# Block sums of the MLP: ended earlier, turned by VectorE and DMA instead of TensorE, with the last down tiles in other PSUM banks and the norm's column sums later

## The chip, the cores and the metric

One core of a Trainium2 chip runs the whole program as one launch. The metric is the device time of that launch in microseconds (us). A profiled execution gives the span from the first to the last instruction, a row for every instruction on every engine, and the waits between them. The engines are TensorE (matmuls; "PE" in the profile, its weight loads "PEld"), VectorE ("DVE"), ScalarE ("ACT"), GpSimd ("POOL", which here only fills buffers and issues DMAs) and SyncE ("SP", which issues the weight loads from memory).

## The reference

A decoder trunk of two layers over 256 positions and 2048 channels, in float32. Layer 0 mixes by dilated attention, layer 1 by sparse attention. Behind each mixer stands an MLP, and behind that a gated embedding ("PLE"):

```python
hn = rmsnorm(h, mlp_norm_g[i])
h = h + jnp.square(jax.nn.relu(hn @ mlp_w1[i])) @ mlp_w2[i]
gate = jax.nn.sigmoid(rmsnorm(h, ple_norm_g[i]) @ ple_w_gate[i])
h = h + (p[i] @ ple_w_proj[i]) * gate
```

The MLP has 8192 hidden channels. The norm divides each position by the root of the mean of its squares over the channels, so it needs a sum over all 2048 channels. At the end a last norm follows.

## The kernel before

**Layout.** The residual stream lies in 16 tiles x[0..15], each 128 channels by 256 positions (channels on the partitions). Every float32 weight is split into a rounded high part and a rest, "whi" and "wlo"; so are the activations. A product is then made of three: high by high, high by low, low by high. ScalarE makes whi (line 281), VectorE wlo (line 308).

**Chunks.** The work is a list of chunks of weights (128 x 1024), written out in order by the program itself; no scheduler reorders it. At each chunk Program.run (line 118) issues, in this order: loads of later chunks on SP, ScalarE's whi of the chunk four ahead, VectorE's wlo of the chunk three ahead, then one stage of every follow-up that is under way (advance(), line 83), then the chunk's matmuls. A follow-up is a Python generator; each `yield` ends a stage. After `yield "tensor"` it goes on behind the matmuls of that chunk. Each engine takes its instructions in the order in which they are issued.

**The MLP** (mlp, line 592). "Up" tiles make 128 hidden channels each; "down" tiles make 128 of the first 1024 output channels from 2048 hidden ones, two chunks a tile. The last 1024 output channels are made by a scheme of seven products of half blocks in place of eight (seven_products, line 649): 32 steps j in three parts, "AD", "B" and "C", which are strewn between the tiles by the loop at line 755. Seven PSUM banks, acc[1..7], collect them over the whole MLP; acc[0] is the one bank that all tiles after the fourth share (mono, line 603). finish (line 684) adds the seven banks to four block sums c11, c21, c12, c22, which have positions on the partitions and channels along the row; they have to be turned to be added to x[8..15].

**PSUM** has four single banks, tag "mm", and two double banks, tag "at" (lines 208 to 212). A slot is given to a new tile of its tag when all instructions of the tile that holds it are behind it, later ones of the program included; of the free slots the one that came free first is taken.

**The end of an MLP.** finish has these stages, one per chunk: the copies of p1 and p5 and the sums u (lines 690 to 693); c11 and c21; c22 and c12; behind the matmuls of that chunk sixteen 128 x 128 turns on TensorE into both double banks (line 708); two stages on, four adds of 128 x 512 to x[8..15] (line 714); then, two tiles a stage, renorm (line 430): high part and squares on ScalarE, low part and the sum of squares on VectorE. Two down-tile chunks follow the last product, then one chunk of the embedding's projection, then the eight chunks of the first gate quarter, of which chunk c needs x[2c] and x[2c+1] as activations.

**The norm behind it** (Norm.factor, line 374) is started after gate chunk 4. When all 16 tiles are summed it issues, each a stage apart: the column sums on TensorE (line 347), the root on VectorE and ScalarE (lines 354 and 355), the inverse and two diagonals on VectorE (lines 361 to 367), and, in layer 0, the spread over all partitions on TensorE (line 371, into the tile of the column sums) and a copy on ScalarE (line 389). In layer 0 the gate quarters are quads, which take four single banks and both double banks in turn (four_banks, line 470); the column sums use a double bank when the quad before used single ones:

```python
ps = banks2()[:, 0, :] if parity[0] else bank()
...
rp = self.spread(ps)
```

Quarter 0 of the gates uses the single banks, the projection of quarter 1 (one chunk) both double banks, quarter 1 the single ones again. In layer 1 (last_ple, line 776) positions are the rows of the gates; column sums and projections use single banks, nothing is spread, and turn (line 782) turns x in four quarters by VectorE's 32 x 32 block transposes and DMAs through memory (regroup, line 312, on GpSimd's queue: one write of 512 KB, then four reads of 128 KB, each of which waits for the write).

Of the kernel before, what the change touches and what calls it, by code (L numbers as in the profile page):

```python
# [10 lines left out]
F32 = mybir.dt.float32  # L11
# [4 lines left out]
P = 128  # L16
D = 2048
T = 256
# [12 lines left out]
ROPE_SWAP = [(j + 16) % 32 for j in range(32)]  # L31

TURN_STAGES = 7
WARM_UP = 9
DMA_AHEAD = 7
DMA_AHEAD_LATER = 10
# [8 lines left out]
def f32(ap):  # L45
    return ap.bitcast(F32)
# [121 lines left out]
def kernel(ctx: ExitStack, tc: tile.TileContext, a: dict, out: bass.AP):  # L168
# [20 lines left out]
    def flip(*args):  # L189
        twos[0] = 4  # L190
        nc.tensor.transpose(*args)  # L191
# [19 lines left out]
    def banks2():  # L211
        return pspool.tile([P, 2, 512], F32, tag="at", name="at", bufs=2)
# [99 lines left out]
    def regroup(dst, src):  # L312

        moved = dram.tile([P, 4, 256], F32, tag="pm", name="pm")
        nc.gpsimd.dma_start(moved, src)
        for b in range(4):
            nc.gpsimd.dma_start(dst[32 * b:32 * b + 32], moved[:, b].rearrange("(a r) x -> r a x", a=4))

    class Norm:
# [51 lines left out]
            mm(ps[:, 128:128 + T], ones, self.diag, start=True, stop=True)  # L371
            return ps[:, 128:128 + T]

        def factor(self, roped=False, spread=True):
            while self.done < KT:
                yield
            yield "tensor"
            ps = self.column([self.acc])
            yield
            self.root(ps)  # L380
            yield
            self.invert()
            if not spread:
                return
            yield "tensor"
            rp = self.spread(ps)
            yield
            r = stat.tile([P, T], F32, tag="sr", name="sr", bufs=1)
            nc.scalar.copy(r, rp)
            if roped:  # L390
                yield
                self.rc = stat.tile([P, T], F32, tag="rc", name="rc", bufs=1)
                self.rs = stat.tile([32, T], F32, tag="rs", name="rs", bufs=1)
                inner, table = (lined, residues) if roped == "residues" else (lined, lined)
                nc.vector.tensor_mul(inner(self.rs), inner(r[:32, :]), table(ropeS))
                nc.vector.tensor_copy(self.rc, r)
                nc.vector.tensor_mul(inner(self.rc[:32, :]), inner(r[:32, :]), table(ropeC))
            self.r = r
# [102 lines left out]
    def single(src, acts, done, mid=(), ring=bank, one_half=False):  # L501

        st = []
        for c in range(2):
            def step(hi, lo, c=c):
                if c == 0:
                    st.append(ring())
                    if ring is not bank:
                        twos[0] = 4
                tiles = [(st[0], i * P, have(acts, 8 * c + i), c + i == 0, 8 * c + i == KT - 1) for i in range(8)]  # L510
                if one_half:
                    for ps, col, rhs, first, end in tiles:
                        three(ps[:, :T], hi, lo, col, rhs, first, end)
                else:
                    mm_tiles(hi, lo, tiles)
                return [done(st[0])] if c else []
            prog.chunk(src(c), step)
            if c == 0:
                for fn in mid:
                    prog.op(fn)  # L520
# [71 lines left out]
    def mlp(layer, xg, norm, to, norm2, pg):  # L592
# [10 lines left out]
        def mono():  # L603
# [5 lines left out]
                acc.extend(bank() for _ in range(4))  # L609
            return acc[{1: 2, 3: 3, 4: 4}.get(opened[0], 0)]  # L610

        def up_done(k, ps, alone=True):
            if alone:
                s = halves(ps)
                t = tmp.tile([P, T], F32, tag="et", name="et", bufs=7)
                nc.vector.tensor_add(t, s[:, :T], s[:, T:])  # L616
            else:
                t = sum_halves(ps)
            yield
            while norm.r is None:  # L620
                yield
            nc.vector.scalar_tensor_tensor(t, t, 0.0, norm.rb, op0=ALU.max, op1=ALU.mult)
            yield
            nc.scalar.activation(t, t, AF.Square)
            ht = cur["h"].tile([P, 2 * T], F32R, tag="h", name="h", bufs=H_BUFS)
            yield from split_to(ht, t)
            h[k] = ht
            kept[k] = t
            if k % 2 == 0:
                return  # L630
            yield
            one, two = kept.pop(k - 1), kept.pop(k)
            a11, a21, a12, a22 = one[:, :P], one[:, P:], two[:, :P], two[:, P:]
            s = cur["h"].tile([P, 2 * T], F32, tag="ew", name="ew", bufs=3)
            d1, s2, s3, s4 = (s[:, i * P:(i + 1) * P] for i in range(4))
            nc.vector.tensor_sub(d1, a21, a22)
            nc.vector.tensor_sub(s3, a11, a21)
            nc.vector.tensor_sub(s2, d1, a11)
            nc.vector.tensor_add(s4, a12, s2)
            if k > 1:  # L640
                yield
            sh = cur["h"].tile([P, 2 * T], F32R, tag="fh", name="fh", bufs=5)
            nc.scalar.copy(sh, s)
            yield
            sl = cur["h"].tile([P, 2 * T], F32R, tag="fl", name="fl", bufs=5)
            nc.vector.tensor_sub(sl, s, f32(sh))
            forms[k // 2] = sh, sl
# [35 lines left out]

        def finish():
            p3, p5, p7, p6, p1, p2, p4 = acc[1:]
            c = cur["h"].tile([P, 2 * CH], F32, tag="r7", name="r7", bufs=R7_BUFS)
            c11, c21, c12, c22 = (c[:, i * 512:(i + 1) * 512] for i in range(4))
            u = cur["h"].tile([P, CH], F32, tag="T", name="T", bufs=1)
            s = cur["h"].tile([P, 2 * CH], F32, tag="r7", name="r7", bufs=R7_BUFS)[:, :512]
            nc.scalar.copy(c11, p1)  # L690
            nc.scalar.copy(s, p5)
            nc.vector.tensor_add(u[:, :512], p6, c11)
            nc.vector.tensor_add(u[:, 512:], p7, u[:, :512])
            yield
            nc.vector.tensor_add(c11, p2, c11)
            nc.vector.tensor_add(c21, p4, u[:, 512:])
            yield
            nc.vector.tensor_sub(c22, s, u[:, 512:])
            nc.vector.tensor_add(c12, p3, s)
            nc.vector.tensor_sub(c12, c12, u[:, :512])  # L700
            yield "tensor"
            flat = []
            for n in range(2):
                flat.append(banks2().rearrange("p a b -> p (a b)"))
                for i in range(4):
                    for m in range(2):
                        src = c[:, (2 * n + m) * 512 + i * P:(2 * n + m) * 512 + (i + 1) * P]
                        flip(flat[n][:, (2 * i + m) * P:(2 * i + m + 1) * P], src, ident)
            yield
            yield  # L710
            for n in range(2):
                for i in range(2):
                    y = xp[4 + 2 * n + i]
                    nc.vector.tensor_add(y, flat[n][:, i * 512:(i + 1) * 512], y)
            begun = []
            for k in range(8, KT + 2, 2):
                for g in begun:
                    for _ in g:
                        pass
                begun = [renorm(i, G_PLE + layer, to, norm2) for i in (k, k + 1) if i < KT]  # L720
                for g in begun:
                    next(g)
                yield
# [13 lines left out]
        def down(b, f):  # L737
            base = layer * 64 + 2 * (b * 8 + f)
            single(lambda c: a["w2d"][base + c], Shifted(h, b * KT), lambda ps: down_done(b, f, ps),
                   ring=mono)  # L740

        quad(lambda c: a["w1"][layer * 128 + c], KT, xg, lambda f, ps: up_done(f, ps, False),
             {4: [norm.factor]}, late=True)
# [5 lines left out]
        parts = [(j, n) for j in range(32) for n in ("AD", "B", "C")]  # L749
        made = {("u", k): -3 for k in range(4)}  # L750
        made.update((what, n) for n, what in enumerate(order))
        first, last = 3, len(order) - 2
        ready = [3 * sum(made["u", 2 * j + 1] <= n - 3 for j in range(32)) for n in range(last + 1)]
        done = downs = 0
        for n, what in enumerate(order):
# [7 lines left out]
                continue  # L763
            spare = min(ready[m] - (m - n) for m in range(n, last + 1) if ready[m] < len(parts) or m == n)
            downs += what[0] == "d"
            even = n - first + 1 + (len(parts) - (last - first + 1)) * downs // (NFB * 8 - 3)
            upto = max(done + 1, min(even, spare)) if n < last else len(parts)
            while done < min(upto, len(parts)):
                j, which = parts[done]
# [6 lines left out]
    def last_ple(layer, pg, xg, norm):  # L776
# [5 lines left out]
        def turn():  # L782
# [3 lines left out]
            e["sq"] = stat.tile([P, 2, 12], F32, name="squares", bufs=1)  # L786
            to = [cur["h"].tile([P, 2 * CH], F32, tag="r7", name="r7", bufs=R7_BUFS) for _ in range(2)]
            for q in range(4):
                for _ in range((1, 3, 3, 11)[q]):
                    yield  # L790
                blocks = cur["h"].tile([P, CH], F32, tag="T", name="T", bufs=1)
                blocks = blocks.rearrange("p (b j k r) -> p b j k r", b=4, j=2, k=4)
# [153 lines left out]
        def gates(q):  # L946
            token_major(lambda c: a["w_gate"][layer * 32 + q * 8 + c], xg,
                        lambda j, ps: gate_done(q, j, ps),
                        {4: [lambda: norm.factor(spread=False)]} if q == 0 else None, banks2 if q else bank)

        prog.op(turn)
        for q in range(2):
# [27 lines left out]
    def ple(layer, pg, xg, norm, nxt, norm2):  # L980
# [34 lines left out]
        for q in range(4):  # L1015
# [12 lines left out]
                prog.op(lambda: parity.__setitem__(0, 0))  # L1028
            else:
                quad(lambda c, q=q: a["w_proj"][layer * 4 + q], 2, pg, proj_done)  # L1030
            hooks = {4: [norm.factor]} if q == 0 else {}
            if q == 3:
                for c in range(6):
                    hooks[c] = [lambda k=k: split_x(k, G_KV, nxt) for k in (2 * c, 2 * c + 1)]
# [721 lines left out]
```

## Time and profile before

| what | us |
|---|---|
| median of 3 runs | 2455.29 |
| lowest, highest | 2454.28, 2455.57 |
| the profiled execution, whole | 2456.09 |
| its span, first to last instruction | 2454.1 |
| TensorE busy in the span | 2443.0 |
| VectorE busy | 2012.8 |
| ScalarE busy | 1507.4 |
| GpSimd busy | 41.9 |

A row of the timelines gives the start in us from the start of the span, the duration in us, the engine, the line of the kernel, the operation, the tile written and those read, their shape, and how many instructions are merged. In square brackets stands how long the engine was idle before, and what released it. Durations of neighbouring matmuls overlap, since they are pipelined; the pace is read from start to start.

### The profile page before, as it was taken

The page shows a single profiled execution, that of the slowest core. Times are in us where ns is not written, and L with a number is a line of the kernel's source. Part 1 is how long each engine was busy: PE and PEld are TensorE (multiplying, and loading weights), DVE is VectorE, ACT ScalarE, POOL GpSimd, SP SyncE. Part 2 cuts the span into 40 slices and gives each one's busy share as a digit, 9 for nine tenths or more (in the row PEclk, how much of TensorE's full clock was granted, in tenths as well). Part 3 has the DMA queues.
Part 4 walks back from the last instruction along what each step waited for, and adds up shares of the span by engine and source line. Part 5 has one row for each costly group of instructions (what it writes and reads, how often), then busy time and mean ns, then how long its engine had stood idle before and what let it go on. Part 6 is the DMA issues. An engine that isn't in the chain of part 4 may idle for free.

```text
span 2454.1 us, 36853 instructions
## 1 busy us (share of the span) xinstructions
PE 2443.0 (100%) x13557; PEld 2117.7 (86%) x13557; DVE 2012.8 (82%) x3562; ACT 1507.4 (61%) x2372; POOL 41.9 (2%) x80
## 2 busy tenths in 40 slices
PE   9999999999999999999999999999999999999998
PEld 8888888888888888888888889988888888888887
DVE  7866687888888888888887989868878888888986
ACT  7544444666566565666664789846656666656654
POOL 0000000000000000000100000000000000000011
PEclk9999999999999999999999999999999999999999
DMA  7666666555565656565565753455655555655566
GB/s 269 204 198 198 198 193 202 181 190 197 198 202 198 200 190 203 192 198 185 194 194 188 245 173 122 130 190 195 198 200 187 192 201 194 201 192 198 194 201 218
DMA packets 133957, 478.68 MB, mean 195 GB/s; under 512 B 15504, under 2 KB 16656, under 8 KB 133776
## 3 DMA queue, kind: packets, MB, share of 16 engines
q1 hardware_dynamic: 128832, 462.22, 57.5%
q0 software_dynamic: 4512, 13.65, 1.9%
q8 instruction: 106, 1.74, 0.3%
q14 instruction: 75, 0.61, 0.1%
q10 hardware_dynamic: 432, 0.46, 0.1%
HBM read 468.40 MB, written 7.86 MB: 194 GB/s over the span
## 4 chain that ended last, share of the span: by engine, by line
PE 98%; DVE 1%; ACT 1%; DMA 0%; issue 0%; SPq 0%; ACTq 0%; DVEq 0%
PE at L450 30%; PE mm L450 17%; PE mm L187 16%; PE at L452 15%; PE at L187 11%; PE mm L452 8%; PE at L191 1%; DMA raw<-in_w_gate 0%; DMA raw<-in_w_v 0%; DVE wlo L308 0%; ACT whi L281 0%; DVE wlo L294 0%; ACT ew L598 0%; DVE z L1337 0%; ACT whi L275 0%
## 5 line engine op out<-in xcount | busy, mean ns | idle before, releaser
L308 DVE TENSOR_TENSOR wlo<-raw,whi 128x1024 fp32r<-128x1024 f32 (+1 forms) x742 | 891.0, 1214 | 109.2 <-PE mm L452 24.9
L281 ACT CAST whi<-raw 128x1024 fp32r<-128x1024 f32 (+1 forms) x741 | 765.6, 1049 | 267.5 <-PE mm L450 85.2
L450 PE MATMUL at<-xa,whi 128*128 128x512 f32 x2016 | 672.9, 394 | 0.0
L450 PE MATMUL mm<-xa,whi 128*128 128x512 f32 x1568 | 533.2, 396 | 0.0
L452 PE MATMUL at<-xa,wlo 128*128 128x256 f32 x2016 | 481.9, 277 | 0.0
L452 PEld LDWEIGHTS at<-xa,wlo 128*128 128x128 f32 x2016 | 378.5, 188 | 41.0
L452 PE MATMUL mm<-xa,wlo 128*128 128x256 f32 x1568 | 398.4, 277 | 0.0
L450 PEld LDWEIGHTS at<-xa,whi 128*128 128x128 f32 x2016 | 353.1, 188 | 50.4
L450 PE MATMUL at<-h,whi 128*128 128x512 f32 x1048 | 349.5, 394 | 0.2
L450 PEld LDWEIGHTS mm<-xa,whi 128*128 128x128 f32 x1568 | 278.9, 188 | 48.8 <-issue 0.4
L452 PEld LDWEIGHTS mm<-xa,wlo 128*128 128x128 f32 x1568 | 294.3, 188 | 19.8
L598 ACT COPY ew<-at 128x512 f32<-128x512 f32 x182 | 106.6, 586 | 260.3 <-PE at L452 251.2
L452 PE MATMUL at<-h,wlo 128*128 128x256 f32 x1048 | 248.5, 277 | 0.0
L452 PEld LDWEIGHTS at<-h,wlo 128*128 128x128 f32 x1048 | 196.8, 188 | 22.5
L450 PEld LDWEIGHTS at<-h,whi 128*128 128x128 f32 x1048 | 182.9, 188 | 26.2 <-ACT ew L598 1.1
L275 ACT CAST whi<-T 128x1024 fp32r<-128x1024 f32 x128 | 134.5, 1051 | 75.7 <-DVE T L303 36.3
L294 DVE TENSOR_TENSOR wlo<-T,whi 128x1024 fp32r<-128x1024 f32 x128 | 155.9, 1218 | 15.2 <-ACT whi L275 15.2
L616 DVE TENSOR_TENSOR et<-ew 128x256 f32<-128x256 f32 x120 | 50.7, 423 | 109.5 <-ACT ew L598 109.5
L187 PE MATMUL mm<-whi,h 128*128 128x512 f32 x416 | 128.7, 391 | 0.0
L187 PE MATMUL mm<-whi,xa 128*128 128x512 f32 (+1 forms) x420 | 126.8, 384 | 0.0
L294 DVE TENSOR_TENSOR wlo<-r,whi 128x1024 fp32r<-128x1024 f32 (+1 forms) x128 | 121.2, 951 | 5.0 <-issue 5.0
L275 ACT CAST whi<-r 128x1024 fp32r<-128x1024 f32 (+1 forms) x128 | 106.7, 835 | 26.9 <-PE at L450 26.9
(355 smaller groups left out, 3320.2 us busy)
## 6 DMA issues: line engine op xcount, KB each, us to landing
raw<-in_w SPq DMA_DIRECT2D x256, 512.0 KB, 4.1
r<-in_w2s SPq DMA_DIRECT2D x128, 512.0 KB, 6.8
raw<-in_w2d SPq DMA_DIRECT2D x128, 512.0 KB, 4.4
raw<-in_w_qk SPq DMA_DIRECT2D x96, 512.0 KB, 4.2
raw<-in_w_gate SPq DMA_DIRECT2D x64, 512.0 KB, 4.3
raw<-in_w_kv SPq DMA_DIRECT2D x48, 512.0 KB, 4.3
raw<-in_w_v SPq DMA_DIRECT2D x46, 512.0 KB, 4.4
raw<-in_w_q SPq DMA_DIRECT2D x32, 512.0 KB, 4.3
```

The costliest lines, as they stand in the source:

```text
L187: nc.tensor.matmul(*args, **kw)
L191: nc.tensor.transpose(*args)
L275: nc.scalar.copy(hi[:, :src.shape[1]], src)
L281: nc.scalar.copy(hi[:, c], t[:, c])
L294: nc.vector.tensor_sub(lo[:, :w], src, f32(hi)[:, :w])
L308: nc.vector.tensor_sub(lo[:, c], t[:, c], f32(hi)[:, c])
L450: nc.tensor.matmul(ps, hi[:, col:col + P], rhs, start=first, stop=False)
L452: nc.tensor.matmul(ps[:, :T], lo[:, col:col + P], rhs[:, :T], start=False, stop=last)
L598: nc.scalar.copy(s, ps)
L616: nc.vector.tensor_add(t, s[:, :T], s[:, T:])
```

## The change

- The products end after down tile 4 of the last block of hidden channels instead of after tile 6, so three tiles follow finish's start instead of one. The 96 parts are spread over two tiles fewer.
- Down tiles 6 and 7 no longer use the shared bank but a double bank, by left_bank.
- finish no longer turns on TensorE. Its two halves are turned by VectorE's block transposes and regroup's DMAs, the first in two tiles of the "fh" ring (so with two writes of 256 KB), the second in the "T" tile; both come back into the "r7" tile, of which s took a part before. The first half is added to x[8..11] three stages after the second half's transposes, the second half to x[12..15] once x[8..11] are through renorm and two more stages are past. The adds are eight of 128 x 256, from SBUF.
- norm.factor waits two stages more, in both layers, before the column sums; the last quarter's turn in last_ple waits two fewer.

```diff
+SUM_STAGES = 3
     def regroup(dst, src):
         moved = dram.tile([P, 4, 256], F32, tag="pm", name="pm")
-        nc.gpsimd.dma_start(moved, src)
+        parts = src if type(src) is list else [src]
+        by = 4 // len(parts)
+        for i, part in enumerate(parts):
+            nc.gpsimd.dma_start(moved[:, i * by:(i + 1) * by], part)
...
-        def factor(self, roped=False, spread=True):
+        def factor(self, roped=False, spread=True, late=0):
             while self.done < KT:
                 yield
+            for _ in range(late):
+                yield
             yield "tensor"
...
-                    if ring is not bank:
+                    if ring.__name__ == "mono":
                         twos[0] = 4
...
+        left = []
+
+        def left_bank():
+            if not left:
+                banks2()
+                two = banks2()
+                left.extend([two[:, 0, :], two[:, 1, :]])
+            return left.pop(0)
...
         def finish():
             p3, p5, p7, p6, p1, p2, p4 = acc[1:]
-            c = cur["h"].tile([P, 2 * CH], F32, tag="r7", name="r7", bufs=R7_BUFS)
+            c, moved = (cur["h"].tile([P, 2 * CH], F32, tag="r7", name="r7", bufs=R7_BUFS) for _ in range(2))
...
+            def turn(n, tiles):
+                by = 4 // len(tiles)
+                src = c[:, n * CH:(n + 1) * CH].rearrange("p (m i b c) -> p m i b c", m=2, i=4, b=4)
+                for i, t in enumerate(tiles):
+                    t = t.rearrange("p (b i m r) -> p b i m r", b=by, i=4, m=2)
+                    for m in range(2):
+                        nc.vector.transpose(t[:, :, :, m].rearrange("p b i r -> p i b r"),
+                                            src[:, m, :, i * by:(i + 1) * by])
+                regroup(turned[n], [t.rearrange("p (b x) -> p b x", b=by) for t in tiles])
+
+            def add(n):
+                src = turned[n].rearrange("p a (i m r) -> p i m a r", i=4, m=2)
+                for i in range(4):
+                    y = x[8 + 4 * n + i].rearrange("p (m a r) -> p m a r", m=2, a=4)
+                    nc.vector.tensor_add(y, src[:, i], y)
...
             nc.vector.tensor_add(c21, p4, u[:, 512:])
+            turn(0, [f32(cur["h"].tile([P, 2 * T], F32R, tag="fh", name="fh", bufs=5)) for _ in range(2)])
             yield
             nc.vector.tensor_sub(c22, s, u[:, 512:])
             nc.vector.tensor_add(c12, p3, s)
             nc.vector.tensor_sub(c12, c12, u[:, :512])
-            yield "tensor"
-            flat = []
-            for n in range(2):
-                flat.append(banks2().rearrange("p a b -> p (a b)"))
-                for i in range(4):
-                    for m in range(2):
-                        src = c[:, (2 * n + m) * 512 + i * P:(2 * n + m) * 512 + (i + 1) * P]
-                        flip(flat[n][:, (2 * i + m) * P:(2 * i + m + 1) * P], src, ident)
-            yield
-            yield
-            for n in range(2):
-                for i in range(2):
-                    y = xp[4 + 2 * n + i]
-                    nc.vector.tensor_add(y, flat[n][:, i * 512:(i + 1) * 512], y)
+            yield
+            turn(1, [cur["h"].tile([P, CH], F32, tag="T", name="T", bufs=1)])
+            for _ in range(SUM_STAGES):
+                yield
+            add(0)
             begun = []
             for k in range(8, KT + 2, 2):
+                if k == 12:
+                    for g in begun:
+                        for _ in g:
+                            pass
+                    begun = []
+                    for _ in range(2):
+                        yield
+                    add(1)
...
         def down(b, f):
-                   ring=mono)
+                   ring=left_bank if (b, f) in ((NFB - 1, 6), (NFB - 1, 7)) else mono)
...
-        first, last = 3, len(order) - 2
+        first, last = 3, len(order) - 4
...
-            even = n - first + 1 + (len(parts) - (last - first + 1)) * downs // (NFB * 8 - 3)
+            even = n - first + 1 + (len(parts) - (last - first + 1)) * downs // (NFB * 8 - 3) + (n == last - 1)
...
-                for _ in range((1, 3, 3, 11)[q]):
+                for _ in range((1, 3, 3, 9)[q]):
...
-                        {4: [lambda: norm.factor(spread=False)]} if q == 0 else None, banks2 if q else bank)
+                        {4: [lambda: norm.factor(spread=False, late=2)]} if q == 0 else None, banks2 if q else bank)
...
-            hooks = {4: [norm.factor]} if q == 0 else {}
+            hooks = {4: [lambda: norm.factor(late=2)]} if q == 0 else {}
```

More of the change, by code (lines that the diff above doesn't have):

```diff
@@ L685, in finish @@
             p3, p5, p7, p6, p1, p2, p4 = acc[1:]
-            c = cur["h"].tile([P, 2 * CH], F32, tag="r7", name="r7", bufs=R7_BUFS)
+            c, moved = (cur["h"].tile([P, 2 * CH], F32, tag="r7", name="r7", bufs=R7_BUFS) for _ in range(2))
             c11, c21, c12, c22 = (c[:, i * 512:(i + 1) * 512] for i in range(4))
             u = cur["h"].tile([P, CH], F32, tag="T", name="T", bufs=1)
-            s = cur["h"].tile([P, 2 * CH], F32, tag="r7", name="r7", bufs=R7_BUFS)[:, :512]
+            s = moved[:, CH:CH + 512]
+            turned = [moved[:, n * CH:(n + 1) * CH].rearrange("p (a x) -> p a x", a=4) for n in range(2)]
+            def turn(n, tiles):
[12 more added lines that the diff above has]
+                    nc.vector.tensor_add(y, src[:, i], y)
             nc.scalar.copy(c11, p1)
```

## The prediction

> **What bounds the kernel now.** I read the page first, then the list of TensorE's waits, then the timelines of TensorE, VectorE, ScalarE and GpSimd around the end of both MLPs.
>
> ```profile
> span 2454.1 us, 36853 instructions
> ...
> PE 2443.0 (100%) x13557; PEld 2117.7 (86%) x13557; DVE 2012.8 (82%) x3562; ACT 1507.4 (61%) x2372; POOL 41.9 (2%) x80
> ...
> PE 98%; DVE 1%; ACT 1%; DMA 0%; issue 0%; SPq 0%; ACTq 0%; DVEq 0%
> ```
>
> ```profile
> PE mm L187 <- DVE ones L219: 1.1, 1, 1.1
> PE at L187 <- DVE whi L279: 0.5, 1, 0.5
> PE at L191 <- DVE r L700: 0.4, 1, 0.4
> PE mm L187 <- DVE et L465: 0.2, 1, 0.2
> ```
>
> 98% of the chain is TensorE, and all its waits (waiting engine and line, what it waited for, us in total) come to 2.2 us in the whole span. So an edit pays only by what it takes out of TensorE's stream, and costs whatever hole it makes there; work on other engines is free until TensorE waits for it.
>
> **Part 1, the sixteen turns of each layer leave TensorE.** TensorE's timeline, layer 0 and then layer 1, in columns start, duration, engine, line:
>
> ```profile
> 1168.27 2.09 PE L191 MATMUL at<-ident,r 128*128 128x128 f32 x16
> 1170.12 0.70 PE L450 MATMUL mm<-xa,whi 128*128 128x512 f32 x2
> ...
> 2346.29 1.03 PE L191 MATMUL at<-ident,r 128*128 128x128 f32 x8
> ...
> 2348.52 0.71 PE L187 MATMUL mm<-whi,xa 128*128 128x512 f32 x2
> ```
>
> From the first turn to the first matmul of the next chunk: 1170.12 - 1168.27 = 1.85 us, and 2348.52 - 2346.29 = 2.23 us, which holds the 0.4 us wait for L700 of the list above. Both vanish: **-4.08 us**. Nothing else leaves the stream, and the products and down tiles that change places stay the same matmuls.
>
> **Part 2, the last three down tiles back to back.** The loop ends the products two tiles earlier than before (after tile 4 instead of 6), so tiles 5, 6, 7 follow without products between. Were all three in the one shared bank, 6 and 7 would wait for the copy of the tile before. They go into the double bank that held p5 and p7, which the first stage of finish() reads while the tile after the products runs:
>
> ```profile
> 1159.85 0.62 PE L450 MATMUL at<-h,whi 128*128 128x512 f32 x2
> 1165.40 0.40 PE L187 MATMUL mm<-h,whi 128*128 128x256 f32 x2
> ```
>
> ```profile
> 1162.34 0.69 DVE L693 TENSOR_TENSOR T<-at,T 128x512 f32<-128x512 f32 x1
> ```
>
> A tile takes 1165.40 - 1159.85 = 5.55 us, and the last of these reads ends 3.2 us into it: cost **0**. Were the other double bank handed out, whose p3 is read behind the new transposes at about t0 + 10, tile 6 would wait 4.5 us; but the bank that is read first is free first.
>
> **Part 3, VectorE carries the turns.** Rows of VectorE, GpSimd, and the summary of L317's DMAs:
>
> ```profile
> 1166.01 1.21 DVE L308 TENSOR_TENSOR wlo<-raw,whi 128x1024 fp32r<-128x1024 f32 x1
> 1167.14 0.68 DVE L698 TENSOR_TENSOR r<-r,T 128x512 f32<-128x512 f32 x1
> ...
> 1169.08 0.43 DVE L727 TENSOR_TENSOR x<-ew,x 128x256 f32<-128x256 f32 x1
> ...
> 1172.89 2.47 DVE L714 TENSOR_TENSOR x<-at,x 128x512 f32<-128x512 f32 x4
> ...
> 1176.41 0.47 DVE L410 SCALAR_TENSOR_TENSOR xa<-x,gains,xa 128x256 fp32r<-128x256 f32 x1
> ...
> 1177.15 0.47 DVE L410 SCALAR_TENSOR_TENSOR xa<-x,gains,xa 128x256 fp32r<-128x256 f32 x1
> ...
> 2366.72 1.42 DVE L794 STREAM_TRANSPOSE T<-x 128x256 f32<-128x256 f32 x4
> ```
>
> ```profile
> 2368.43 0.54 POOL L315 DMA_DIRECT2D pm<-T  x1 [83.11 <-DVE sz L362]
> 2373.83 2.20 POOL L317 DMA_DIRECT2D r<-pm  x4 [4.85 <-PE mm L187]
> ...
> 2384.14 0.56 POOL L315 DMA_DIRECT2D pm<-T  x1 [7.55 <-DVE T L794]
> 2387.73 2.21 POOL L317 DMA_DIRECT2D r<-pm  x4 [3.03 <-DMA pm<-T]
> ...
> 2392.38 0.56 POOL L315 DMA_DIRECT2D pm<-T  x1 [1.88 <-DMA raw<-in_w_proj]
> 2400.81 2.21 POOL L317 DMA_DIRECT2D r<-pm  x4 [7.87 <-DMA raw<-in_w_gate]
> ```
>
> ```profile
> DMA to landing us min/median/max: 3.9/6.0/8.3
> ```
>
> The first half is turned by four transposes: 1.42 us. The second, two of twice the width, costs between 1.42/2 (fixed cost per instruction only) and 1.42 (elements only): I take 1.35. Eight adds of 128x256 replace four of 128x512 (2.47 us): at 0.38 each they are 3.0, bounded by 8 x 0.3 and 8 x 0.68. Per layer VectorE gets about 3.3 us more, and the DMAs two writes of 512 KB and eight reads of 128 KB more.
>
> Does TensorE notice? Count from t0, the start of down tile 5 (which plays the part of 1159.85), chunks at 2.775 us. VectorE has c11 and c21 done at t0 + 6.16 (the 1166.01 row). Until add(0) it then does four transposes 1.42, five weight subtractions at 1.13 (1166.01 to 1167.14), three sums 1.94 (1167.14 to 1169.08), two transposes 1.35, and of two tiles the adds (2 x 0.86) and norm steps (2 x 0.74, from 1176.41 to 1177.15): 13.6 us, so it comes to add(0) at **t0 + 19.8**. The second write of the first half is issued 0.29 us after the transposes (2368.14 to 2368.43), at t0 + 7.9. Write to first read took 5.40, 3.59 and 8.43 us in the rows above; the fourth read is issued 1.65 us after the first and lands a median of 6.0 us later (the last row, of L317's DMAs). So the data stand at 7.9 + 5.4 + 1.65 + 6.0 = **t0 + 20.9**, between 17.0 and 26.2: VectorE waits w = 1.1 us, between 0 and 6.4. What is queued behind add(0) on VectorE is the weight subtractions, the norm steps and the low halves of x; ScalarE's copies of x[8..] wait with it. VectorE then has adds 3.0, tile 7's adds 0.9, six subtractions 6.8 and nine norm steps 6.7: it ends x[15] at t0 + 37.2 + w. TensorE needs that tile at gate chunk 7, at t0 + 6 x 2.775 + 2.87 + 7 x 2.775 = 38.9. The cover is 1.7 us, so w = 1.1 costs **0**. The column sums would have stood after chunk 5 (t0 + 36.2), 1.0 + w too early; two chunks later they are covered. The second half has seven chunks for the same journey and is never late.
>
> **Part 4, the column sums two chunks later, and what they are now late for.** In layer 0 the column sums take a double bank ("at"), and keep it until the spread and its copy, two chunks on. There are two of these. Before, columns follow gate chunk 5, the spread follows chunk 7, and the projection of the next quarter comes after that and takes both double banks, four 128-row outputs:
>
> ```profile
> 1186.85 0.50 PE L187 MATMUL at<-ones,acc 128*128 128x1 f32 x4
> 1187.21 0.70 PE L450 MATMUL mm<-xa,whi 128*128 128x512 f32 x2
> ...
> 1188.69 0.63 PE L450 MATMUL mm<-xa,whi 128*128 128x512 f32 x2
> ...
> 1192.86 0.59 PE L187 MATMUL at<-diag,ones 128*128 128x256 f32 x2
> 1193.10 0.81 PE L450 MATMUL at<-h,whi 128*128 128x512 f32 x2
> ```
>
> After the change the columns follow chunk 7, and the spread follows the first gate chunk of the next quarter. The projection lies between them, with one double bank free. Its outputs 2 and 3 must take the bank of outputs 0 and 1, once these are read; those reads are issued one stage later, and TensorE, which takes its instructions in order, stands until then. From the start T of the columns:
>
> ```profile
> 1188.61 0.16 DVE L361 RECIPROCAL sy<-sz 128x2 f32<-128x2 f32 x1
> ...
> 1189.39 0.48 DVE L367 TENSOR_SCALAR diag<-ident,col 128x128 f32<-128x128 f32 x2
> ...
> 1195.76 0.75 DVE L465 TENSOR_TENSOR et<-mm,es 128x256 f32<-128x256 f32 x2
> ```
>
> ```profile
> 1187.58 0.20 ACT L355 ACTIVATE sz<-sv 128x2 f32<-128x2 f32 x1 [2.37 <-DVE sv L354]
> ...
> 1193.76 1.21 ACT L463 COPY es<-mm 128x256 f32<-128x256 f32 x4
> ```
>
> The root's ScalarE step ends at T + 0.93 (1187.78 - 1186.85). The four copies of gate quarter 0 follow, 1.21 us, to T + 2.14; VectorE's four sums start when the first copy is done, about T + 1.3, and at 0.75 for two end at T + 2.8. Then, in VectorE's order: a weight subtraction, 1.13, to T + 3.9; the inverse and diagonals, 1189.87 - 1188.61 = 1.26, to T + 5.1 or 5.2; the sums of outputs 0 and 1, 0.75, to T + 5.85. Without the shortage outputs 2 and 3 begin after the columns and two pairs, 1188.69 - 1186.85 = T + 1.84. The hole is **+4.0 us**. Its bounds: 1.7, if subtraction and inverse did not stand in front (2.8 + 0.75 - 1.84), and 5.2, if one more weight step of 1.2 does. I take 4.0, since VectorE's order there is fixed by the program.
>
> In layer 1 the columns take a single bank, and only the root reads it. The next projection's second output gets that bank. TensorE is there 0.37 + 3 x 0.23 = 1.05 us after T (a 512-column matmul is 5.55/16 x 2/3 = 0.23); VectorE comes to the root at t0 + 37.2 + w and four more steps (three subtractions, q=0's transposes), 42.0 + w, against T + 1.05 = t0 + 42.2. With w between 0 and 1.1 the wait is 0 to 1.1: **+0.5 us**. The last quarter's turn, two stages earlier, has slack on both sides and is worth 0.
>
> **The sum.** Against the profiled execution (2456.09 us, 2.0 us beside its span of 2454.1): -4.08 + 4.0 + 0.5 = +0.4, so 2456.5. That execution lies 0.8 us above the median of the runs, 2455.29, which gives **2455.7**.
>
> **The rivals.**
>
> *A: the hole isn't there*, if a bank is found for outputs 2 and 3 or their partners are read in time. For it: no wait for a PSUM bank of this kind stands in the list of waits. Against: in the rows above the columns (1186.85), spread (1192.86) and projection (1193.10) all write "at", of which the program has two. Time 2455.29 - 4.08 = 2451.2.
>
> *B: the first half's blocks land late* (the slower side). VectorE stands at add(0), and from w = 1.7 on TensorE waits for x[15] at gate chunk 7. For it: the third GpSimd pair took 8.43 us, and reads up to 8.3. Against: all of it must come together. At w = 6.4 the price is 4.7 us a layer: 2460.4 with one layer, 2465.1 with both.
>
> *C: the hole also slows TensorE after it.* The first matmuls of the kernel, after a start in which TensorE had only small ones and a wait:
>
> ```profile
> 5.74 1.28 PE L187 MATMUL at<-whi,xa 128*128 128x512 f32 x2 [0.47 <-DVE whi L279]
> ...
> 9.97 0.81 PE L187 MATMUL at<-whi,xa 128*128 128x512 f32 x2
> ```
>
> Nine matmuls took 9.97 - 5.74 = 4.23 us where the rate of the rest gives 9 x 0.23 = 2.1: a loss of 2.1 us. After the hole the same would make 2457.8. The Trainium skill speaks for this one ("TensorE: Matmul & The Clock Gate", Part 1): an idle window of 3.4 us halves the clock until a busy window has passed, and the windows run free. By that rule, as an estimate, an idle stretch of 4.0 us holds a whole window in about one case of six; the trace before has no hole in mid-kernel to try it on.
>
> **How the numbers follow.** Forecast 0.60 (its own range 2453 to 2457.5, the bounds of the hole), A 0.20, C 0.10, B 0.10. A range of 2450.5 to 2460 holds A, C and the forecast and leaves out most of B. A change under 0.2% (4.9 us, about what a measurement of this kernel can tell from none) covers all but B and the lucky edge of A (where over 0.8 us more than the turns is saved): faster 0.07, same 0.84, slower 0.09.
>
> **What would show it.** Right: no L191 turns at the end of the MLPs; in layer 0, within the projection after gate quarter 0, TensorE idle about 4 us, released by VectorE's sum at L465; the first gate chunk directly behind the projection. Wrong: that projection without a gap (A), matmuls at 0.4 us spacing behind it (C), gate chunk 7 waiting for x tiles while VectorE waits for the turned blocks (B), or the first half of tile 6 waiting for a bank.

## The result, and the profile after

The changed kernel is slower: a median of 2469.51 us (2467.50 to 2471.77) against 2455.43 us before (2454.28 to 2455.66) on the same chip, a ratio of 1.0058 with a 95% interval of 1.0045 to 1.0071. That is 14.1 us or 0.6% more, and 9.5 us above the upper end of the predicted range. The profiled execution took 2470.67 us, 14.58 more than the one of before (2456.09).

First the page of the changed kernel: span, busy times, and the shares of the chain that ended last.

```profile
span 2468.9 us, 36868 instructions
...
PE 2446.3 (99%) x13525; PEld 2118.7 (86%) x13525; DVE 2021.9 (82%) x3582; ACT 1508.4 (61%) x2372; POOL 54.0 (2%) x102
...
PE 95%; DVE 2%; ACT 1%; DMA 1%; issue 0%; SPq 0%; ACTq 0%; DVEq 0%
```

TensorE has 32 instructions fewer, which are the turns of the two layers, and still was busy 3.3 us longer. Its share of the chain fell from 98% to 95%. The list of its waits (waiting line, what it waited for, us in total, times, the longest) says why:

```profile
PE at L456 <- ACT ew L604: 7.8, 2, 4.2
PE at L456 <- DVE h L1055: 4.3, 1, 4.3
```

Both rows are new. The second is the hole that the prediction put into layer 0's projection. The first is two waits for ScalarE's copies of down tiles. TensorE's timeline shows the three places, in order of time: down tile 7 of layer 0, the projection of quarter 1, down tile 7 of layer 1.

```profile
1158.39 0.28 PE L458 MATMUL at<-h,wlo 128*128 128x256 f32 x1
1162.33 0.50 PE L456 MATMUL at<-h,whi 128*128 128x512 f32 x1 [3.66 <-ACT ew L604]
...
1196.59 0.40 PE L458 MATMUL at<-h,wlo 128*128 128x256 f32 x2
1201.29 1.19 PE L456 MATMUL at<-h,whi 128*128 128x512 f32 x2 [4.30 <-DVE h L1055]
...
2348.15 0.28 PE L458 MATMUL at<-h,wlo 128*128 128x256 f32 x1
2352.59 0.79 PE L456 MATMUL at<-h,whi 128*128 128x512 f32 x1 [4.16 <-ACT ew L604]
```

From start to start, less the 0.11 us (0.23 for the pair of two) that the first instruction needs, the holes cost 3.83, 4.47 and 4.33 us. The instruction behind two of them is longer than it should be, and so are those that follow. The view by stretches of time shows it. It is cut here at the moments at which the granted clock changes; the columns are the stretch, its length and TensorE's busy time with the number of rows, the granted clock, the DMA share and GB/s.

```profile
1156.63:1160.05 3.42, 2.03 (x12) 1.00 0.80 272
1160.05:1163.46 3.41, 1.14 (x6) 1.00 0.70 168
1163.46:1166.87 3.41, 3.41 (x13) 0.50 1.02 353
...
1194.19:1197.60 3.41, 2.80 (x18) 1.00 0.48 157
1197.60:1201.01 3.41, 0.00 (x0) 1.00 0.29 85
1201.01:1204.42 3.41, 3.13 (x10) 0.50 0.17 68
1204.42:1207.83 3.41, 3.41 (x20) 1.00 0.00 0
2347.89:2351.30 3.41, 0.54 (x4) 1.00 0.92 286
2351.30:2354.71 3.41, 2.12 (x7) 0.50 0.81 211
2354.71:2358.12 3.41, 3.41 (x12) 0.50 1.03 315
```

Behind each hole the clock is halved for one or two stretches of 3.41 us. At the halved clock a pair of one 512-column and one 256-column matmul takes 0.64 us from start to start (1164.11 and 1164.75), at the full clock about 0.35, so 45% of TensorE's busy time in these stretches is lost: 0.453 x (3.41 + 3.13) = 2.96 us in layer 0, 0.453 x (2.12 + 3.41) = 2.51 us in layer 1.

The two timelines can be compared in parts, between the column sums (L188 here, L187 before) that the change doesn't move and the last matmul. Of the kernel before:

```profile
491.89 0.50 PE L187 MATMUL at<-ones,acc 128*128 128x1 f32 x4
...
1284.82 0.50 PE L187 MATMUL mm<-ones,acc 128*128 128x1 f32 x4
...
1670.07 0.50 PE L187 MATMUL at<-ones,acc 128*128 128x1 f32 x4
...
2444.97 0.28 PE L187 MATMUL mm<-wlo,xa 128*128 128x256 f32 x1
```

And of the changed one:

```profile
490.86 0.50 PE L188 MATMUL at<-ones,acc 128*128 128x1 f32 x4
...
1295.04 0.50 PE L188 MATMUL mm<-ones,acc 128*128 128x1 f32 x4
...
1680.28 0.50 PE L188 MATMUL at<-ones,acc 128*128 128x1 f32 x4
...
2459.74 0.28 PE L188 MATMUL mm<-wlo,xa 128*128 128x256 f32 x1
```

| us | layer 0 | layer 1 |
|---|---|---|
| turns gone | -1.85 | -2.23 |
| hole before down tile 7 | +3.83 | +4.33 |
| hole in the projection | +4.47 | 0 |
| half clock behind the holes | +2.96 | +2.51 |
| sum | +9.41 | +4.61 |
| measured: 804.18 - 792.93, 779.46 - 774.90 | +11.25 | +4.56 |

The terms explain layer 1 within 0.1 us. Layer 0 has 1.8 us more, which the last section comes to. Between the layers nothing changed (385.24 and 385.25), and the start took 1.0 us less.

### The profile page after: what moved, and what is told of

Same layout as the page of the kernel before. It is cut to its first block, busy times and chain, and to the rows that moved or that the text cites. A ratio compares the mean times of both kernels' runs of the same rounds, so it can differ in the third digit from the quotient of the medians.

```text
span 2468.9 us, 36868 instructions
## 1 busy us (share of the span) xinstructions
PE 2446.3 (99%) x13525; PEld 2118.7 (86%) x13525; DVE 2021.9 (82%) x3582; ACT 1508.4 (61%) x2372; POOL 54.0 (2%) x102
## 4 chain that ended last, share of the span: by engine, by line
PE 95%; DVE 2%; ACT 1%; DMA 1%; issue 0%; SPq 0%; ACTq 0%; DVEq 0%
PE at L456 29%; PE mm L456 16%; PE mm L188 16%; PE at L458 15%; PE at L188 11%; PE mm L458 8%; DVE wlo L309 1%; PE at L192 1%; DVE wlo L295 0%; ACT whi L282 0%; DMA raw<-in_w2d 0%; DMA x<-in_xT 0%; ACT whi L276 0%; ACT ew L604 0%; DVE T L303 0%
## 5 line engine op out<-in xcount | busy, mean ns | idle before, releaser
L456 PE MATMUL at<-h,whi 128*128 128x512 f32 x1048 | 355.9, 399 | 12.2 <-ACT ew L604 7.8
L604 ACT COPY ew<-at 128x512 f32<-128x512 f32 x182 | 106.5, 585 | 259.3 <-PE at L458 247.6
L458 PE MATMUL at<-h,wlo 128*128 128x256 f32 x1048 | 253.8, 280 | 0.0
L188 PE MATMUL mm<-whi,h 128*128 128x512 f32 x416 | 128.8, 391 | 0.0
L188 PE MATMUL mm<-whi,xa 128*128 128x512 f32 (+1 forms) x420 | 126.6, 384 | 0.0
```

The lines of the kernel that those rows point to most:

```text
L188: nc.tensor.matmul(*args, **kw)
L456: nc.tensor.matmul(ps, hi[:, col:col + P], rhs, start=first, stop=False)
L458: nc.tensor.matmul(ps[:, :T], lo[:, col:col + P], rhs[:, :T], start=False, stop=last)
L604: nc.scalar.copy(s, ps)
```

## The experiments

**Where the two holes before tile 7 come from.** In layer 0, VectorE first and then ScalarE:

```profile
1154.75 1.42 DVE L713 STREAM_TRANSPOSE fh<-r 128x256 f32<-128x256 f32 x4
...
1157.79 0.69 DVE L733 TENSOR_TENSOR r<-at,r 128x512 f32<-128x512 f32 x1
```

```profile
1158.51 0.58 ACT L604 COPY ew<-at 128x512 f32<-128x512 f32 x1 [5.75 <-DVE r L733]
...
1161.70 0.57 ACT L604 COPY ew<-at 128x512 f32<-128x512 f32 x1
```

L733 is the sum that reads p3. Tile 5's bank is the other half of p3's double bank, and the program orders all accesses to one double bank, a read after a read in its other half too: ScalarE's copy of tile 5, whose own matmuls had ended at 1153.0, waits 5.75 us for L733. The copy of tile 6 stands three microseconds behind it in ScalarE's queue (1161.70). Tile 6 and tile 7 are again two halves of one double bank, so tile 7 waits for that copy. Theory: the lost time is these hand-overs of banks, the hole of the projection, and the halved clock behind each. Its main rival: the added transposes and DMAs slow TensorE down directly.

**Tiles 6 and 7 in single banks.**

```diff
-                   ring=left_bank if (b, f) in ((NFB - 1, 6), (NFB - 1, 7)) else mono)
+                   ring=bank if (b, f) in ((NFB - 1, 6), (NFB - 1, 7)) else mono)
```

> The changed kernel, but down tiles 6 and 7 take single banks (those of p1 and p6, read in the first stage of finish()) in place of the two halves of one double bank. Theory (the time went into holes at bank hand-overs and into the half pace behind each): both waits before tile 7 (start to start 3.83 us in layer 0, 4.33 in layer 1) and the slow stretches behind them (1.6 and 2.4) vanish: 2469.5 - 12.1 = 2457.4, and the list of waits keeps only the 4.3 us in layer 0's projection. Rival 1 (the half pace comes from the added transposes and DMAs, not from the holes): only the holes go, 2469.5 - 8.2 = 2461.3, and pairs at 0.64 us remain around tile 7. Rival 2 (ScalarE's copies are late, whatever the bank): the wait moves to the gates' first banks, and the time stays at 2469.

2464.98 us, ratio 1.0039 (1.0024 to 1.0054). TensorE's waits:

```profile
PE at L456 <- DVE h L1055: 4.3, 1, 4.3
PE mm L188 <- ACT ew L604: 2.1, 1, 2.1
PE mm L456 <- ACT ew L604: 1.4, 1, 1.4
```

The waits before tile 7 are gone, so it was the shared double bank. But only 4.5 us are won, not 12.1. The first gate chunks now wait for the same copies, and the 2.1 us in layer 1 halved the clock again. Rival 2 was right for that part: ScalarE's copies are late, and whoever needs the bank next finds it out.

**The spread in a bank of its own.**

```diff
-            rp = self.spread(ps)
+            rp = self.spread(banks2()[:, 0, :])      # in layer 0 only
```

> The changed kernel, but in layer 0 the spread takes a double bank of its own one stage later, so the column sums' bank is free once the root has read it, instead of being held until the spread is copied. Theory: the hole in the projection of quarter 1 (4.47 us start to start) shrinks to the root's read (below 1 us), and with it goes the slow stretch behind it (1.4): 2469.5 - 5.9 = 2463.6, up to 2464.6. Rival 1 (half pace not from the hole): 2469.5 - 4.5 = 2465.0 with pairs at 0.64 us still there. Rival 3 (outputs 2 and 3 wait for the sums of the gate before, not for the column's bank): 2469.5.

2465.13 us, ratio 1.0040 (1.0025 to 1.0055): the theory's upper figure is 0.5 us lower, and rival 1's 2465.0 is nearer. The first row of the waits, and stretches of 3.41 us around tile 7 of layer 0:

```profile
PE at L456 <- ACT ew L604: 7.3, 2, 3.7
```

```profile
1157.23:1160.64 3.41, 1.62 (x10) 1.00 0.90 309
1160.64:1164.05 3.41, 1.47 (x8) 1.00 0.66 162
1164.05:1167.46 3.41, 3.41 (x13) 0.50 1.02 353
```

The wait for L1055 is gone, and no half clock stands at the projection any more, which rival 1 needed there. So that hole was the double bank that the columns held, and the clock there was halved by the hole. Before tile 7 both stay. The stretches bound the condition: 1.79 us idle out of 3.41 (3.41 - 1.62) left the clock alone, 1.94 (3.41 - 1.47) halved it.

**Both edits.**

> The changed kernel with both edits: tiles 6 and 7 in single banks, and the spread in a double bank of its own. Theory: no hole is left, and the turns of TensorE are still gone: 2469.5 - 12.1 - 5.9 = 2451.5, which is 3.9 below before. Rival 1: 2469.5 - 8.2 - 4.5 = 2456.8, because half-pace stretches remain. Rival 4 (without the holes VectorE has 6 us less until the column sums in layer 0, and comes late with x[15] or the sums): a new wait of TensorE on VectorE at gate chunk 7 or at the column sums, 1 to 4 us, 2452.5 to 2455.5.

2458.53 us, ratio 1.0014 (1.0005 to 1.0024): still slower than before, and 7.0 us above the theory. Rival 4 had the size, 1 to 4 us, but neither the place nor the engine:

```profile
PE mm L456 <- ACT ew L604: 2.2, 1, 2.2
PE mm L188 <- ACT ew L604: 2.1, 1, 2.1
```

No hole of 3.5 us is left, but the waits at the first gate chunks are, 2.39 and 2.22 us from start to start. In the profiled execution (2456.89) neither halved the clock, so the half pace of rival 1, whose figure of 2456.8 it meets, isn't there; the ten executions spread from there to 2462.03.

**One part of the change alone, on the kernel before.**

```diff
-            hooks = {4: [norm.factor]} if q == 0 else {}
+            hooks = {4: [lambda: norm.factor(late=2)]} if q == 0 else {}
```

> The kernel before, with one part of the change alone: layer 0's column sums two chunks later, on the same bank as before. Theory: the hole of the projection (4.3 to 4.5 us) and a slow stretch behind it (1.4) appear, with no block sum moved, no transpose and no DMA added: 2455.4 + 5.9 = 2461.3. Rival 1: the hole alone, 2455.4 + 4.5 = 2459.9, pairs at 0.347 us behind it. If the hole came from VectorE's new work it would be shorter or absent: 2455.4 to 2458.

2463.42 us, ratio 1.0032 (1.0020 to 1.0045). TensorE's timeline in the projection:

```profile
1192.72 0.40 PE L454 MATMUL at<-h,wlo 128*128 128x256 f32 x2
1197.42 1.19 PE L452 MATMUL at<-h,whi 128*128 128x512 f32 x2 [4.30 <-DVE h L1024]
```

The hole is 4.30 us long as in the changed kernel, without a transpose or a DMA added, and the clock is halved behind it while the DMA engines moved 20 GB/s (1197.40 to 1200.80). The rival is out for this place. The cost is 8.3 us, not 5.9: here the half clock lasted two stretches, and the matmuls afterwards had the slower pace of the last section.

**Which tile's bank is wanted too early.**

```diff
-                   ring=left_bank if (b, f) in ((NFB - 1, 6), (NFB - 1, 7)) else mono)
+                   ring=left_bank if (b, f) == (NFB - 1, 7) else bank if (b, f) == (NFB - 1, 6) else mono)
```

> The spread in a double bank of its own, and of the last two down tiles only tile 6 in a single bank; tile 7 in the double bank that p5 and p7 left. With both tiles in single banks TensorE waited 2.2 us (layer 0) and 2.1 us (layer 1) at the first gate chunks for the copy of a down tile: on ScalarE the copy of tile 7 stands behind a norm step that waits for VectorE's block sums (add(0) at 1167.80). Theory: it is tile 7's bank that the gates want too early, and the double bank is asked for only by the next projection, so both waits vanish: 2456.9 (the profiled execution of both edits, with no slow stretch) - 2.39 - 2.22 = 2452.3, its runs as close together as those of before. Rival 2 (some bank is always wanted too early): a wait of 1 to 2 us for tile 6's copy at the same place, 2454 to 2456.

> The mirror of the kernel with tile 6 alone in a single bank: now tile 6 in the double bank and tile 7 in a single one. Theory: no wait before tile 7, but the gates' wait for tile 7's copy stays, 2.2 us in layer 0 and 2.1 in layer 1: 2456.9 with no slow stretch, 2458.5 in the median as with both tiles in single banks. Rival 2 (the number of single banks held decides, not which tile holds them): no wait, 2452.3.

With tile 6 single: 2455.66 us, ratio 1.0001 (0.9992 to 1.0010), 3.4 us above the theory. With tile 7 single: 2457.80, ratio 1.0013 (1.0004 to 1.0022), with waits of 2.5 and 2.2 us for L604 as expected. In layer 1 the theory holds, the wait goes with tile 7's bank. In layer 0 it fell. The wait stayed, under another name:

```profile
PE mm L456 <- ACT h L1045: 2.5, 1, 2.5
```

```profile
1168.10 0.50 ACT L412 ACTIVATE xa<-x,gains 128x256 fp32r<-128x256 f32 x1
...
1169.53 0.56 ACT L604 COPY ew<-at 128x512 f32<-128x512 f32 x1
1169.99 1.06 ACT L1045 COPY h<-mm 128x512 f32<-128x512 f32 x2
```

L1045 are the copies of the first projection, whose matmuls had ended at 1166.7. They stand behind two norm steps and two squares (1168.10 to 1169.53), which need the first block sums of VectorE (from 1167.37). It is ScalarE's queue that is late. In this execution ScalarE didn't stand still for add(0): until 1167.15 it waited for a weight load, and the norm steps' own 1.43 us came on top. With both tiles in single banks it had stood still for add(0), 0.68 us.

**The transposes behind the sum that reads p3.**

```diff
             nc.vector.tensor_add(c21, p4, u[:, 512:])
-            turn(0, ...)
             yield
             nc.vector.tensor_sub(c22, s, u[:, 512:])
             nc.vector.tensor_add(c12, p3, s)
             nc.vector.tensor_sub(c12, c12, u[:, :512])
+            turn(0, ...)
             yield
```

> The changed kernel with the four transposes of the first half behind the sums of c22 and c12 instead of ahead of them; banks as in the changed kernel. Theory: the sum that reads p3 ends 1.42 us sooner, so tile 5's and tile 6's copies and tile 7 do: the holes before tile 7 shrink from 3.66 and 4.16 us to 2.2 and 2.7, the hole in the projection stays 4.3. In time 2469.5 - 2.84 = 2466.7 if both slow stretches stay, 2462.7 if both go. The runs so far put the halving of the clock at the end of a window of 3.41 us in which TensorE stood still for more than about half (1.76 us idle: no, 1.97 us: yes); by that a hole of 2.2 us halves it in about half of the executions and one of 2.7 us in two of three, so the runs scatter between the two figures. Rival 5 (only a window that is idle throughout halves the clock): no slow stretch before tile 7, always 2462.7 to 2463. Rival 6 (the holes have nothing to do with the transposes): 2469.5.

2470.40 us, ratio 1.0063 (1.0049 to 1.0077): a miss, and rival 6's figure for another reason. ScalarE around tile 6's copy:

```profile
1157.31 0.59 ACT L604 COPY ew<-at 128x512 f32<-128x512 f32 x1 [4.57 <-DVE r L732]
...
1160.13 0.51 ACT L412 ACTIVATE xa<-x,gains 128x256 fp32r<-128x256 f32 x1 [1.29 <-DVE x L761]
...
1161.79 0.57 ACT L604 COPY ew<-at 128x512 f32<-128x512 f32 x1
```

Tile 5's copy came 1.2 us sooner, as expected. Tile 6's did not (1161.79 against 1161.70). Ahead of it on ScalarE stands a norm step that needs tile 5's sum in x (L761), and VectorE made that sum behind the transposes again. The 1.42 us of transposes were in the way by either order. Rival 5 is out too: the windows before tile 7 were idle for 3.33 and 2.55 us, not throughout, and both halved the clock.

**Layer 0's first block sums one stage later, with the edits so far.**

```diff
-            for _ in range(SUM_STAGES):
+            for _ in range(SUM_STAGES + 1 - layer):
```

> Tile 6 in a single bank, tile 7 in a double one, the spread in a double bank of its own, and in layer 0 the first block sums (add(0)) one stage later. With the first three edits TensorE waited 2.5 us at layer 0's first gate chunk for ScalarE's copies of the first projection, and halved its clock behind it in some executions; ScalarE had these copies behind two norm steps that waited for add(0) (its first sum at 1167.37, the copies at 1169.99). Theory: one stage later the copies stand ahead of those norm steps and the wait is gone; the column sums, which had 7 us to spare (last sum of squares at 1185.73, columns at 1193.06), still don't wait. Then no hole is left and the turns' 4.08 us stand alone: 2455.1 - 4.1 = 2451.0, with runs as close together as those of before. Rival 7 (ScalarE is late by its own amount of work): a wait of 1 to 2.5 us remains at that place, 2452 to 2455.

> The same with add(0) one stage later in both layers. Theory: layer 1 had no wait at its first gate chunk, so nothing is won there; the root of its column sums, which VectorE read 0.44 us late, comes behind up to one more stage of work: 2451.0 to 2452.5. Rival 8 (VectorE in layer 1 has a stage to spare): the same time as with layer 0 alone, 2451.0.

> All four edits with the block sums one stage later still: add(0) two stages later than in the changed kernel in layer 0, one in layer 1. Theory 9: ScalarE's copies don't stand behind add(0) any more, so a further stage changes nothing there, 2453.1 to 2453.3 as with one stage less. Rival 11 (ScalarE and VectorE are still crowded by the block sums in the slower executions): less scatter and 1 to 1.5 us less, 2452.

2453.28 us, ratio 0.9995 (0.9986 to 1.0003); with both layers one stage later 2453.09, ratio 0.9992 (0.9983 to 1.0001); with one stage more 2453.04, the same ratio and interval. The first one's longest wait is the one at the start that the kernel before has too:

```profile
PE mm L188 <- DVE ones L220: 1.1, 1, 1.1
```

No hole is left, and the profiled execution took 2452.15, 3.94 below the one of before. But the medians are only 1.6 to 2.1 us lower, and each interval ends just above 1: these versions are no longer slower, and whether they are faster is not settled. The theory's 2451.0 wasn't reached. Nor was rival 11's 2452 with one stage more, but that version has a new wait:

```profile
PE mm L456 <- DVE xa L416: 1.2, 1, 1.2
```

A gate chunk of layer 0 waits 1.2 us there for the low half of an x tile of the second block sums, so this run doesn't settle whether the crowding matters.

**A second profile of two kernels.**

> A second profile of the kernel with all four edits (tile 6 single, tile 7 double, spread on its own, layer 0's first block sums one stage later), whose first profile had no hole and was 3.9 us under the profile of before, while the medians differ by only 1.6. Theory 9 (a margin near zero: ScalarE's copies of the first projection end within a few tenths of the moment the gates want the banks, and in slower executions they end later): an execution above 2453 shows a wait of 0.5 to 2 us at layer 0's first gate chunk. Rival 10 (the difference lies in parts that the change doesn't touch): no wait there, and the stretch between the column sums at 491 us and 1284 us is 791.0 to 792.0 us, as in the first profile (791.6).

> A second profile of the kernel before, unchanged. In the first one the stretches between column sums were 792.9 us (491.9 to 1284.8) and 774.9 (1670.1 to the last matmul at 2444.97), and the start ahead of the first column sums took 54.9. Rival 10: the two stretches are the same here within 0.3 us, and what differs between executions is the start and the stretch of the attention.

2455.53 us for the kernel with all four edits, 2455.66 for the kernel before, both on another chip than the first profile of the four edits. The slower execution has no wait at layer 0's first gate chunk, so theory 9 fell. Between its column sums it took 793.2 us (491.35 to 1284.56) where the first profile had 791.6. Rival 10 is right that no wait stands there, but it had put that stretch at 791.0 to 792.0 and the difference outside: 1.6 of the 3.4 us lie inside, in matmuls whose instructions the change doesn't touch, and 1.4 in layer 1's stretch. One stretch of layer 0's gates, in the first and in the second profile of that same program:

```profile
1210.00:1275.00 65.00, 65.00 (x377) 1.00 0.59 189
```

```profile
1210.00:1275.00 65.00, 65.00 (x370) 1.00 0.56 186
```

TensorE is always busy, the granted clock is 1.00, and yet 2% fewer instructions fit into the same 65 us. The chip alone isn't the reason, since the first profile has both paces within it (last section). The kernel before repeated its stretches within 0.2 us (792.9 and 774.7 in its second profile).

## Why the prediction was wrong, step by step

**Part 1 was right.** All turns at the end of the MLPs are gone, and nothing else left the stream.

**Part 2 is the step that failed.** "The bank that is read first is free first" held for tile 6, which started without a wait. The part asked only for tile 6, and priced both tiles at 0. Tile 7 goes into the other half of the same double bank and waits for the copy of tile 6. That copy is queued on ScalarE behind the copy of tile 5, and this one behind VectorE's L733 and the new transposes. The profile of before had a trace of it, in the list of ScalarE's waits: its copies of down tiles waited for that same sum there, 9.1 us in two waits, at no cost since no tile followed.

```profile
ACT ew L598 <- DVE r L699: 9.1, 2, 4.6
```

The price in the changed kernel is 3.83 + 4.33 us without the clock. The Trainium skill ("PSUM — Partial Sum Buffer", PSUM bank collisions raise a hardware error) has engines kept apart by bank, reads against reads too; the program here keeps them apart by whole double banks, and the removal of the sharing in the first experiment shows that this is what tile 7 waited for.

**Part 3 was right in its sizes and wrong in what it called covered.** The transposes took 1.42 and 1.30 us (estimate 1.35), four adds 1.43 (0.36 each, estimate 0.38). VectorE was at add(0) at 1168.10, that is t0 + 20.9 with t0 = 1147.23, and didn't wait for the blocks, so rival B did not happen:

```profile
1161.06 1.30 DVE L713 STREAM_TRANSPOSE T<-r 128x512 f32<-128x512 f32 x2
...
1168.10 1.43 DVE L721 TENSOR_TENSOR x<-r,x 128x256 f32<-128x256 f32 x4
```

It named ScalarE's norm steps as waiting with add(0), and not what stands behind them in ScalarE's queue: the copies of tile 7 and of the first projection, whose banks the gates want. In the changed kernel the holes hid this. With the holes filled it cost 2.1 to 2.5 us at each place, until the sums came a stage later.

**Part 4 was right.** The hole is 4.30 us against 4.0 predicted (1.7 to 5.2), released by the sums of outputs 0 and 1 (L1055) as its working said; the line that it named as the sign, L465, is the sum of the gates, not of the projection. Undoing the cause removed the hole. Layer 1's 0.5 us didn't show in the changed kernel; with layer 1's hole gone, two profiles have it, 0.4 and 0.5 us for the root's first step.

**Rival C came true at all three holes**, and its odds were the second failure. It had one case in six for a hole of 4.0 us, on the condition that a whole window is idle. The stretches show that a window of 3.41 us needs to be idle for only about 1.9 us, and so a hole of 4 us always has one (split evenly over two windows, it leaves 2.0 us in each). Its price was 2.1 us for one hole; the three cost 5.5 together. By the Trainium skill ("TensorE: Matmul & The Clock Gate", Part 1) the window is 3.4 us and runs free, and the traces agree: the three halvings stand 37.55 and 1150.29 us apart, 11 and 337 times 3.413. Where it has an idle window as the condition, the measurement decides for a little over half of one.

In the sum, +0.4 was made of -4.08, +4.0 and +0.5. What was missing is 8.2 for tile 7, 5.5 for the clock, and 1.8 in layer 0 that the table leaves open.

## What to carry to other kernels

When a tile gets a bank, look not only at who must have read it, but at who shares its allocation, and follow each reader back through its own engine's queue to what that engine waits for; do it for every tile that is moved, and once more with the holes filled, since a hole hides the next late engine. In these traces a hole of 2.5 us or more in TensorE's stream cost about 1.4 to 2.6 us beyond its own length through the halved clock, and one of 2.1 to 2.2 us did so at times, so two short waits can be cheaper than one long one. Work that moves from the bounding engine to a busy one is only as free as the queues behind it are short: here 4.1 us of turns were saved and 18.1 us of holes and half clock paid, and with the holes filled about 2 us were won at best, which the runs don't settle.

## What was not expected of the hardware

**The clock is halved by a window that is a little over half idle.** In the profiles of all the runs, between the first and the last 20 us, fourteen windows of 3.413 us at full clock in which TensorE stood idle for 1.94 us (the shortest) to 3.41 us were all followed by half clock; those with up to 1.79 us idle were not. A window at half clock that had 1.12 to 1.33 us idle (four kernels) was followed by another one; 0.28 us idle ended it. Where between 1.79 and 1.94 us the limit lies wasn't tried.

**Two paces at full clock.** In stretches without a wait and at granted clock 1.00, a pair of one 512-column and one 256-column matmul takes either 0.347 or 0.353 us from start to start, and keeps that pace for tens of us (the 377 and 370 rows above). One program had both in two executions, and the first of these had both within it: 0.353 in layer 0's first gate quarter, 0.347 in the later ones. The kernel before had 0.347 in layer 0's gates, in both its profiles. The changed kernel had the slower one in layer 0 in tiles 5 and 6 and in the gates, while tile 7, behind its hole, was back at the faster one:

```profile
1210.00:1275.00 65.00, 65.00 (x370) 1.00 0.56 180
```

From the projection of quarter 2 to the last column sums the same matmuls took 66.56 us before (1218.26 to 1284.82) and 67.85 here (1227.19 to 1295.04): 1.29 us, most of the 1.8 us that the table above leaves open. What sets the pace is open: it followed a hole at times, and at times came without one. It is also the likeliest reason why the version without holes won less than its 4.1 us, but that is argued, not shown.
